# Feed-forward start of a decoder trunk: input block sums from two temporaries and a wide buffer, and their place in VectorE's queue

## The chip, the core and the metric

The kernel runs on one core of a Trainium2 chip. The metric is the time of one execution on the device in microseconds (us); the median of three runs is 2041.17 us (2040.91 to 2041.41). A profile of one further execution gives the rows that are quoted. PE is TensorE (its weight loads are PEld), DVE is VectorE, ACT is ScalarE, POOL is GpSimd, SP is the engine whose queue issues most DMAs. L475 is line 475 of the kernel before.

## What is computed

Two layers on a sequence of 512 tokens of width 1024, all in 32-bit floats. A layer is a half-step SwiGLU feed-forward block, a mixer (a convolution module in layer 0, sparse attention in layer 1), a second feed-forward block and a gated embedding; each block begins with an RMS norm.

```python
def rms_norm(x, g):
    return x * lax.rsqrt(jnp.mean(x * x, axis=-1, keepdims=True) + RMS_EPS) * g

def swiglu(x, wg, wu, wd):
    return (jax.nn.silu(x @ wg) * (x @ wu)) @ wd

for i in range(DEPTH):                       # DEPTH = 2
    x = x + 0.5 * swiglu(rms_norm(x, ffn1_norm[i]), ffn1_w_gate[i], ffn1_w_up[i], ffn1_w_down[i])
    ...                                      # conformer_conv or nsa_mixer
    x = x + 0.5 * swiglu(rms_norm(x, ffn2_norm[i]), ffn2_w_gate[i], ffn2_w_up[i], ffn2_w_down[i])
    ...                                      # gated embedding
```

The hidden width is 2816, which is 22 tiles of 128 columns. There are four feed-forward blocks in all: two in each layer.

## The kernel before

Activations lie transposed, features on the 128 partitions and 512 tokens along the row: `xs[k]`, k from 0 to 7, is 128 features of the residual stream. To keep 32-bit accuracy every operand is split into a high half, rounded by a copy on ACT, and a low half, the difference, taken on DVE; a product is then three matmuls, high x high, high x low and low x high (`mm3`, L349 to L351). Weight tiles of 128x1024 are loaded by SP's queue into `raw` (two buffers) or `rawx` (two buffers), then split into `wh` (ACT, L291 or L309) and `wl` (DVE, L292 or L310); there are five buffers of each. `ahead` (L327 on) does the loads and splits up to five steps before the product that uses them. The norm's factor is not applied to the inputs: the sum of squares runs along (`square_sum`, the running sum `acc` at L425), `rfin` sums it over features on PE (L438), adds the epsilon on DVE (`v`, L460, kept as `self.vins`), takes the power on POOL, spreads the row on PE and copies it to `R` on ACT (L451), and `R` scales the results.

A feed-forward block (`ffn`) takes its hidden tiles in three parts of 8, 8 and 6. Tiles 0 and 1 of the first part are plain: each has a gate and an up product of 8 input tiles. Their results are scaled by `R` (L576), go through SiLU on ACT (L577) into a temporary of tag `t` (four buffers), are multiplied (L551) and split (L553, L554). The SiLU frees one of the eight PSUM banks, the split another.

All other tiles go in pairs (`pairs`), with a scheme of the Strassen-Winograd kind: the product of a 2x2 block of weights with a 2x2 block of inputs is made from 7 products of half size instead of 8. It needs sums of weight blocks and sums of input blocks.

- Weight sums, per pair and once for gate and once for up. `_split` with kind "a" takes the first weight tile's halves (L291, L292) and calls `first_sums`, which makes `sq` (L320), a sum in `rawx` (L321) and its halves `s1hl` (L323, L324). `combine` with "c" and "d" makes the other two sums (L305, L306) and splits them (L309, L310). L305 and L306 read what the others wrote.
- Input sums, once per block: `right_sums` is called four times, for k = 0 to 3, and makes the four sums T1 to T4 of input tiles k and k+4. It scales the two tiles by the norm's gain on ACT (L473) into two temporaries `a` and `b`, makes `t12` and `t34` with four subtractions of 256 columns on DVE (L475 `t<-...`), and splits each into a `px` tile of 1024 (high half L483 on ACT, low half L475 `px<-t,px` on DVE). All four temporaries have tag `t`. The first pair needs them: its products run plain weights x inputs first (four), then T2 and T1, then T3, then T4.

`first_sums` of the first pair is called while tile 0's plain products are written out, that of the second pair when the first pair's are. Two calls of `right_sums` stand behind tile 0's products, two behind tile 1's, each within `issue_after(self.vins)`.

The order on each engine's queue is not the written order. A planner simulates the program and gives each engine the ready instruction that was written first; a `high_priority` block counts as written earlier. Within `issue_after(ins)`, the instructions that run on the engine of `ins` are queued behind it, without a wait for its end; instructions on other engines are free. Each engine then works through its queue in order, waiting by semaphores. A tag's buffers are used in turn, and a new tile waits for the users of the one that had its place.

The pairs' outputs are evicted from PSUM into tiles of tag `G`, 128x1024, three buffers (L496 on ACT, L495 on DVE): two for each pair.

Of the kernel before, what the change touches and what calls it, by code (L numbers as in the profile page):

```python
# [3 lines left out]

# [1 line left out]

# [5 lines left out]
F32 = mybir.dt.float32  # L12
F32R = mybir.dt.float32r
I32 = mybir.dt.int32
AF = mybir.ActivationFunctionType
OP = mybir.AluOpType
# [4 lines left out]
KD, FT = D // 128, DFF // 128  # L21
# [29 lines left out]
G, HPG, HD, KV, QD = 4, 4, 64, 256, 1024  # L51
# [143 lines left out]
class Kern:  # L195
# [72 lines left out]
    def _split(self, what, j):  # L268
        nc = self.nc
        w = sum(x[2] for x in UNITS[j])  # L270
        if what == "r":
            t = self.wpool.tile([128, HU], F32, name=f"wr{j}", tag="wh", bufs=self.HLB)
            nc.sync.dma_start(t[:, :w], self.a["w"][j, :, :w])
            self.hl[j] = (t, t)
            return
        if what in "cd":
            self.combine(what, j)
            return
        pair = KINDS[j] == "a"
        t = self.raw[j]  # L280
        if KINDS[j] == "s":
            del self.raw[j]
        h, l = self.halves()
        name = UNITS[j][0][0][0]
        nsa, calm = name.startswith("nsa"), name.startswith(CALM)
        eng = nc.gpsimd if calm or nsa and j % 4 in L_POOL else nc.vector
        for c in self.pieces(j, w):
            if nsa and j % 4 in H_POOL:
                nc.gpsimd.tensor_copy(h[:, c], t[:, c])
            else:  # L290
                nc.scalar.activation(h[:, c], t[:, c], AF.Copy)  # L291
            eng.tensor_tensor(l[:, c], t[:, c], h[:, c].bitcast(F32), op=OP.subtract)  # L292
        self.hl[("s", j) if pair else j] = (h, l)
        if pair:
            self.first_sums(j)

    def combine(self, what, j):

# [169 lines left out]
    def right_sums(self, name, i, k):  # L468

        nc = self.nc  # L470
        a, b, t12, t34 = (self.tmp() for _ in range(4))
        for t, kk in ((a, k), (b, k + 4)):
            nc.scalar.activation(t, self.xs[kk], AF.Copy, scale=self.col(name, i * KD + kk))  # L473
        lo, hi = slice(0, 256), slice(256, 512)
        sub = lambda o, x, y: nc.vector.tensor_tensor(o, x, y, op=OP.subtract)  # L475
        sub(t12[:, lo], a[:, hi], a[:, lo])
        sub(t12[:, hi], b[:, hi], t12[:, lo])
        sub(t34[:, lo], b[:, hi], a[:, hi])
        sub(t34[:, hi], b[:, lo], t12[:, hi])
        T = []  # L480
        for t in (t12, t34):
            p = self.ptile("px", 8, HU, F32R)
            nc.scalar.activation(p[:, :512], t, AF.Copy)  # L483
            sub(p[:, 512:], t, p[:, :512].bitcast(F32))
            T += [(p[:, :256], p[:, 512:768]), (p[:, 256:512], p[:, 768:])]
        self.T4.append(T)

    def pairs(self, names, i, f):
# [47 lines left out]
    def ffn(self, n, i, nxt):  # L536
        nc = self.nc
        X = self.X
        g, u, d = (f"ffn{n}_w_{s}" for s in ("gate", "up", "down"))
        self.now, self.T4 = (f"ffn{n}", i), []  # L540
        fin = self.rfin(self.acc)

        def plain(p, nm, f, ks=range(KD)):
            for k in ks:
                self.mm3(p, self.block((nm, i, k, f)), X[k], k == 0, k == KD - 1)

        for pi, fs in enumerate(PARTS):
            hid = {}

            def gated(f, gr, pu):  # L550
                nc.vector.tensor_tensor(pu, pu, gr, op=OP.mult)  # L551
                h, l = self.ptile("hid", HIDS, dt=F32R), self.ptile("hid", HIDS, dt=F32R)
                nc.scalar.activation(h, pu, AF.Copy)  # L553
                nc.vector.tensor_tensor(l, pu, h.bitcast(F32), op=OP.subtract)  # L554
                hid[f] = (h, l)

            if pi == 0:
                assert PLAIN == 2
                wait = []
                for f in range(PLAIN):  # L560
                    pg, pu = self.bank(), self.bank()
                    for ks in (range(KD - 1), (KD - 1,)) if f == 0 else (range(KD),):
                        plain(pg, g, f, ks)
                        if f == 1:
                            next(fin)
                        plain(pu, u, f, ks)
                    wait.append((f, pg, pu))
                    if f == 0:
                        next(fin)
                    with self.tc.issue_after(self.vins):  # L570
                        for k in (2 * f, 2 * f + 1):
                            self.right_sums(f"ffn{n}_norm", i, k)
                R = self.R
                for f, pg, pu in wait:
                    gr = self.tmp()
                    nc.vector.tensor_tensor(pg, pg, R, op=OP.mult)  # L576
                    nc.scalar.activation(gr, pg, AF.Silu)  # L577
                    gated(f, gr, pu)
            for f in fs[::2]:
                if f < PLAIN:  # L580
                    continue
                both = self.pairs((g, u), i, f)
                G = next(both)
                nc.vector.tensor_tensor(G, G, R[:, None, :].to_broadcast([128, 2, 512]), op=OP.mult)
                nc.scalar.activation(G, G, AF.Silu)
                U = next(both)
                drain(both)
                for h in range(2):
                    gated(f + h, G[:, h], U[:, h])
                self.skew_next()  # L590
                self.skew_next()
            last = pi == len(PARTS) - 1
            if last:
                self.prep_start(*nxt)
            for ms in ((0, 1), *((m,) for m in range(2, KD))):
                p = {m: self.bank() for m in ms}
                if len(ms) > 1:
                    self.held = {ENTRY[PLACE[d, i, f, m][0]] for f in fs for m in ms}
                for part in (fs[:-2], fs[-2:]):
                    for m in ms:  # L600
                        for f in part:
                            self.mm3(p[m], self.block((d, i, f, m)), hid[f], f == fs[0], f == fs[-1])
                self.held = set()
                for m in ms:
                    nc.vector.scalar_tensor_tensor(p[m], p[m], 0.5, R, op0=OP.mult, op1=OP.mult)  # L605
                    nc.vector.tensor_tensor(self.xs[m], p[m], self.xs[m], op=OP.add)
                    if last:
                        self.prep(m)
# [72 lines left out]
    def taps(self, c):  # L681

        T = [self.ptile("tw", TWB, 128 * LAGS) for _ in range(PH)]
        for q in range(PH):
            self.nc.sync.dma_start(T[q], self.a["tw"][CONV_ON[:c].count("pe"), q])
        return T

# [818 lines left out]
```

## Time and profile before

| | |
|---|---|
| median of three runs | 2041.17 us (2040.91 to 2041.41) |
| the profiled execution | 2038.98 us, its span 2037.2 us |
| PE busy | 1998.5 us, 98% of the span |
| DVE busy | 1564.8 us, 77% |
| ACT busy | 1102.2 us, 54% |
| POOL busy | 329.9 us, 16% |
| `wl<-raw,wh` on DVE (L292), 128x1024 | 203 x 1233 ns |
| `px<-t,px` on DVE (L475), 128x512 | 32 x 686 ns |
| `t<-...` on DVE (L475), 128x256 | 64 x 420 ns |

A row of a timeline gives the start and duration in us, the engine, the line, the operation, the tile written and the tiles read, and the size; in brackets stand the idle time of the engine just before it and what ended that. A row of a group gives the number of instructions, their busy time in us and the mean in ns of one. A row of a stretch gives the stretch in us, its length, then the busy time of each engine with the number of its instructions, the granted clock of PE (1.00 is full speed), the busy share of the DMA engines and the rate in GB/s. An instruction's duration includes its latency: on DVE and ACT the next one starts before it ends.

### The profile page before, as it was taken

The page shows a single profiled execution, that of the slowest core. Times are in us where ns is not written, and L with a number is a line of the kernel's source. Part 1 is how long each engine was busy: PE and PEld are TensorE (multiplying, and loading weights), DVE is VectorE, ACT ScalarE, POOL GpSimd, SP SyncE. Part 2 cuts the span into 40 slices and gives each one's busy share as a digit, 9 for nine tenths or more (in the row PEclk, how much of TensorE's full clock was granted, in tenths as well). Part 3 has the DMA queues.
Part 4 walks back from the last instruction along what each step waited for, and adds up shares of the span by engine and source line. Part 5 has one row for each costly group of instructions (what it writes and reads, how often), then busy time and mean ns, then how long its engine had stood idle before and what let it go on. Part 6 is the DMA issues. An engine that isn't in the chain of part 4 may idle for free.

```text
span 2037.2 us, 32829 instructions
## 1 busy us (share of the span) xinstructions
PE 1998.5 (98%) x12534; PEld 1794.0 (88%) x12534; DVE 1564.8 (77%) x2767; ACT 1102.2 (54%) x1972; POOL 329.9 (16%) x365
## 2 busy tenths in 40 slices
PE   8999999999999999999999999999999989999998
PEld 6989999888789898988899989888888779898987
DVE  8869777795687796877977868647989797786875
ACT  6636445663565363545644535437888665363543
POOL 0000000352200000021000000557666200000022
PEclk9999999999999999999999999999999999999999
DMA  4323323466325243243232322463332023232241
GB/s 168 104 93 103 125 75 103 180 213 204 125 98 172 92 143 118 96 144 104 83 114 94 114 91 89 159 189 108 90 93 100 27 98 114 94 115 93 88 142 61
DMA packets 79484, 235.16 MB, mean 115 GB/s; under 512 B 8848, under 2 KB 16160, under 8 KB 79328
## 3 DMA queue, kind: packets, MB, share of 16 engines
q1 hardware_dynamic: 78368, 230.69, 34.2%
q8 instruction: 98, 1.61, 0.3%
q0 software_dynamic: 816, 2.33, 0.3%
q14 instruction: 58, 0.48, 0.1%
q10 hardware_dynamic: 144, 0.07, 0.0%
HBM read 214.66 MB, written 16.29 MB: 113 GB/s over the span
## 4 chain that ended last, share of the span: by engine, by line
PE 83%; DVE 9%; ACT 3%; issue 2%; DMA 2%; SPq 0%; POOL 0%; DVEq 0%; ACTq 0%; POOLq 0%
PE b L349 26%; PE b L350 26%; PE b L351 26%; PE b L797 2%; DMA raw<-in_w 1%; DVE t L1221 1%; DVE wl L292 1%; PE b L1156 1%; PE b L1095 1%; DVE t L475 1%; DVE s L408 1%; DVE wl L310 1%; PE b L1218 1%; DVE e L1174 1%; ACT e L1176 0%
## 5 line engine op out<-in xcount | busy, mean ns | idle before, releaser
L349 PE MATMUL b<-s,wh 128*128 128x256 f32 (+1 forms) x1408 | 451.3, 322 | 8.3 <-ACT t L577 6.9
L350 PE MATMUL b<-s,wh 128*128 128x256 f32 (+1 forms) x1408 | 449.8, 320 | 1.3 <-DVE s L408 0.9
L351 PE MATMUL b<-s,wl 128*128 128x256 f32 (+1 forms) x1408 | 449.0, 320 | 0.1
L291 ACT ACTIVATE wh<-raw 128x1024 fp32r<-128x1024 f32 (+1 forms) x251 | 263.9, 1054 | 259.1 <-PE b L350 170.0
L349 PE MATMUL b<-px,wh 128*128 128x256 f32 (+1 forms) x1112 | 321.1, 290 | 6.0 <-ACT px L483 6.0
L350 PE MATMUL b<-px,wh 128*128 128x256 f32 (+1 forms) x1112 | 321.9, 290 | 2.3 <-DVE px L475 2.3
L351 PE MATMUL b<-px,wl 128*128 128x256 f32 (+1 forms) x1112 | 321.6, 290 | 0.0
L292 DVE TENSOR_TENSOR wl<-raw,wh 128x1024 fp32r<-128x1024 f32 (+1 forms) x205 | 251.4, 1228 | 74.9 <-ACT wh L291 74.2
L349 PEld LDWEIGHTS b<-s,wh 128*128 128x128 f32 x1408 | 270.1, 192 | 28.4 <-ACT t L577 7.8
L350 PEld LDWEIGHTS b<-s,wh 128*128 128x128 f32 x1408 | 270.3, 192 | 19.9 <-DVE s L408 2.2
L351 PEld LDWEIGHTS b<-s,wl 128*128 128x128 f32 x1408 | 270.0, 192 | 17.7 <-DVE wl L292 0.5
L351 PE MATMUL b<-hid,wl 128*128 128x512 f32 x704 | 275.3, 393 | 0.0
L350 PE MATMUL b<-hid,wh 128*128 128x512 f32 x704 | 275.1, 392 | 0.0
L349 PE MATMUL b<-hid,wh 128*128 128x512 f32 x704 | 270.4, 390 | 0.0
L292 POOL TENSOR_TENSOR wl<-raw,wh 128x1024 fp32r<-128x1024 f32 (+1 forms) x53 | 128.4, 2427 | 717.2 <-ACT wh L291 717.1
L349 PEld LDWEIGHTS b<-px,wh 128*128 128x128 f32 x1112 | 209.5, 189 | 10.9 <-ACT px L483 6.4
L350 PEld LDWEIGHTS b<-px,wh 128*128 128x128 f32 x1112 | 209.8, 189 | 7.5 <-DVE px L475 2.7
L351 PEld LDWEIGHTS b<-px,wl 128*128 128x128 f32 x1112 | 209.5, 189 | 3.8
L496 ACT ACTIVATE G<-b 128x256 f32<-128x256 f32 x400 | 145.0, 376 | 124.2 <-PE b L351 102.6
L605 DVE SCALAR_TENSOR_TENSOR b<-b,R 128x512 f32<-128x512 f32 x96 | 66.4, 694 | 120.3 <-PE b L351 120.3
L350 PEld LDWEIGHTS b<-hid,wh 128*128 128x128 f32 x704 | 132.3, 188 | 28.8
L349 PEld LDWEIGHTS b<-hid,wh 128*128 128x128 f32 x704 | 132.3, 188 | 28.6
(246 smaller groups left out, 3716.2 us busy)
## 6 DMA issues: line engine op xcount, KB each, us to landing
raw<-in_w SPq DMA_DIRECT2D x255, 512.0 KB, 3.3
rawx<-in_w SPq DMA_DIRECT2D x80, 512.0 KB, 3.2
tw<-in_tw SPq DMA_DIRECT2D x20, 576.0 KB, 6.7
skew<-table SPq DMA_DIRECT2D x16, 320.0 KB, 5.6
z<-t SPq DMA_DIRECT2D x16, 256.0 KB, 2.2
hid<-z SPq DMA_DIRECT2D x16, 256.0 KB, 4.1
tt<-skew SPq DMA_DIRECT2D x16, 256.0 KB, 3.0
wr<-in_w SPq DMA_DIRECT2D x8, 512.0 KB, 4.0
```

The source lines that it names most:

```text
L291: nc.scalar.activation(h[:, c], t[:, c], AF.Copy)
L292: eng.tensor_tensor(l[:, c], t[:, c], h[:, c].bitcast(F32), op=OP.subtract)
L310: nc.vector.tensor_tensor(l, src, h.bitcast(F32), op=OP.subtract)
L349: mm(out, sh, mh, start=start, stop=False, **how)
L350: mm(out, sh, ml, start=False, stop=False, **how)
L351: mm(out, sl, mh, start=False, stop=stop, **how)
L408: b = nc.vector.scalar_tensor_tensor(view(l), x, g, view(h.bitcast(F32)), op0=OP.mult, op1=OP.subtract)
L475: sub = lambda o, x, y: nc.vector.tensor_tensor(o, x, y, op=OP.subtract)
L496: copy = lambda o, x: nc.scalar.activation(o, x, AF.Copy)
L605: nc.vector.scalar_tensor_tensor(p[m], p[m], 0.5, R, op0=OP.mult, op1=OP.mult)
L797: nc.tensor.matmul(p[:, q * SP:q * SP + SP], T[q][:, d * 128:d * 128 + 128], u[:, q, o:o + SP], start=d == 0, stop=d == LAGS - 1)
L1095: nc.tensor.matmul(P[mh][:, :124], w, B[kk // 4][:, kk % 4, :], start=kk == 0, stop=kk == 15)
```

## The change

Three things change.

`right_sums` scales its two input tiles into the two halves of one tile of tag `G`, 1024 wide, and holds its sums in two temporaries instead of two inputs and two sums in four. The sums are laid out as T1 beside T3 and T2 beside T4. T1 and T3 are each a difference of neighbouring blocks, so one subtraction of 512 columns over a strided view makes both; T2 and T4 take one of 256 each. The splits into `px` are as before. The last low half's instruction is kept as `self.righted`.

The four calls stand within `issue_after(self.vins)` only in the very first feed-forward block; in the other three they are free.

From the time that all four calls are written out in a block (`len(self.T4) == 4`), the DVE instructions of `_split` for a pair's first tile (L292) and all DVE instructions of `first_sums` (L320, L321, L324) are queued behind `self.righted`. The first pair's are written before that and stay free; the second pair's are the first that this holds.

```diff
@@ _split
-            eng.tensor_tensor(l[:, c], t[:, c], h[:, c].bitcast(F32), op=OP.subtract)
+            with self.behind() if pair else nullcontext():
+                eng.tensor_tensor(l[:, c], t[:, c], h[:, c].bitcast(F32), op=OP.subtract)
         self.hl[("s", j) if pair else j] = (h, l)
         if pair:
-            self.first_sums(j)
+            with self.behind():
+                self.first_sums(j)
+
+    def behind(self):
+
+        return self.tc.issue_after(self.righted) if len(self.T4) == 4 else nullcontext()
@@ right_sums
-        a, b, t12, t34 = (self.tmp() for _ in range(4))
-        for t, kk in ((a, k), (b, k + 4)):
-            nc.scalar.activation(t, self.xs[kk], AF.Copy, scale=self.col(name, i * KD + kk))
+        ab, t13, t24 = self.ptile("G", 3, 1024), self.tmp(), self.tmp()
+        for n, kk in enumerate((k, k + 4)):
+            nc.scalar.activation(ab[:, n * 512:n * 512 + 512], self.xs[kk], AF.Copy, scale=self.col(name, i * KD + kk))
         lo, hi = slice(0, 256), slice(256, 512)
         sub = lambda o, x, y: nc.vector.tensor_tensor(o, x, y, op=OP.subtract)
-        sub(t12[:, lo], a[:, hi], a[:, lo])
-        sub(t12[:, hi], b[:, hi], t12[:, lo])
-        sub(t34[:, lo], b[:, hi], a[:, hi])
-        sub(t34[:, hi], b[:, lo], t12[:, hi])
-        T = []
-        for t in (t12, t34):
+        cut = lambda t: t.rearrange("p (h c) -> p h c", h=2)
+        sub(cut(t13), cut(ab)[:, :, hi], cut(ab[:, :512]))
+        sub(t24[:, lo], ab[:, 768:], t13[:, lo])
+        sub(t24[:, hi], ab[:, 512:768], t24[:, lo])
+        T = [None] * 4
+        for n, t in enumerate((t13, t24)):
             p = self.ptile("px", 8, HU, F32R)
             nc.scalar.activation(p[:, :512], t, AF.Copy)
-            sub(p[:, 512:], t, p[:, :512].bitcast(F32))
-            T += [(p[:, :256], p[:, 512:768]), (p[:, 256:512], p[:, 768:])]
+            self.righted = nc.vector.tensor_tensor(p[:, 512:], t, p[:, :512].bitcast(F32), op=OP.subtract).ins
+            T[n], T[n + 2] = ((p[:, c], p[:, 512 + c.start:512 + c.stop]) for c in (lo, hi))
@@ ffn
+                first = (n, i) == (1, 0)
...
-                    with self.tc.issue_after(self.vins):
+                    with self.tc.issue_after(self.vins) if first else nullcontext():
                         for k in (2 * f, 2 * f + 1):
                             self.right_sums(f"ffn{n}_norm", i, k)
```

More of the change, by code (lines that the diff above doesn't have):

```diff
@@ L2 @@
 import math
-from contextlib import ExitStack
+from contextlib import ExitStack, nullcontext
 import numpy as np
```

## The prediction

> **What bounds the kernel now.** I read the page first, then the busy time of TensorE in stretches of 20 us, then the timeline of PE, DVE and ACT where PE had gaps. PE is busy nearly all the span, so only its gaps and its slow clock are for sale. Apart from the attention layer and the last 17 us they lie at one place: the start of each of the four feed-forward blocks, where PE goes from the plain products to the first pair. I call these starts A (first block of layer 0), B (second block of layer 0), C and D (the same of layer 1). The stretches, with the columns PE, PEld, DVE, ACT, POOL, clock, DMA share, GB/s:
>
> ```profile
> span 2037.2 us, 32829 instructions
> ...
> 20.00:70.00 50.00, 43.76 (x288) 40.38 (x288) 46.96 (x75) 33.04 (x52) 1.14 (x1) 0.90 0.30 96
> 560.00:625.00 65.00, 63.77 (x418) 57.34 (x417) 58.11 (x91) 41.54 (x67) 1.71 (x2) 1.00 0.36 118
> 960.00:1010.00 50.00, 45.31 (x283) 41.44 (x282) 41.82 (x71) 30.52 (x48) 1.12 (x1) 0.93 0.20 67
> 1640.00:1680.00 40.00, 34.81 (x236) 32.40 (x236) 38.08 (x65) 26.36 (x43) 1.13 (x1) 0.96 0.25 79
> ```
>
> DVE is busy 46.96 of 50 us in A and 38.08 of 40 in D: at these starts DVE, not PE, carries the load. The gaps themselves, from PE's timeline (start, duration, then in brackets the idle time ahead and what ended it): first the wait for A's norm, which the change leaves alone, then two rows of A, one of B, three of C, two of D:
>
> ```profile
> 22.53 1.05 PE L438 MATMUL b<-meanr,acc 128*128 128x1 f32 x8 [2.08 <-DVE acc L425]
> ...
> 50.12 0.80 PE L349 MATMUL b<-px,wh 128*128 128x256 f32 x2 [3.44 <-ACT px L483]
> ...
> 52.06 0.58 PE L349 MATMUL b<-s,wh 128*128 128x256 f32 x1 [0.72 <-ACT t L577]
> ...
> 602.77 0.39 PE L349 MATMUL b<-s,wh 128*128 128x256 f32 x1 [1.14 <-ACT t L577]
> ...
> 989.85 0.39 PE L350 MATMUL b<-px,wh 128*128 128x256 f32 x1 [0.99 <-DVE px L475]
> ...
> 993.59 0.51 PE L349 MATMUL b<-px,wh 128*128 128x256 f32 x2 [2.54 <-ACT px L483]
> ...
> 995.50 0.58 PE L349 MATMUL b<-s,wh 128*128 128x256 f32 x1 [1.17 <-ACT t L577]
> ...
> 1662.00 0.39 PE L350 MATMUL b<-px,wh 128*128 128x256 f32 x1 [1.29 <-DVE px L475]
> ...
> 1667.11 0.58 PE L349 MATMUL b<-s,wh 128*128 128x256 f32 x1 [3.90 <-ACT t L577]
> ```
>
> Every gap but the first waits for the right sums (their high halves, L483, or low halves, L475) or for the SiLU of the plain products (L577), which frees a PSUM bank. Idle: A 3.44 + 0.72 = 4.2 us, B 1.1, C 0.99 + 2.54 + 1.17 = 4.7, D 1.29 + 3.90 = 5.2; 15.2 together. PE first ran dry at 50.12 - 3.44 = 46.7 in A, 989.85 - 0.99 = 988.9 in C and 1662.00 - 1.29 = 1660.7 in D. Behind the gaps PE runs at half clock, in steps of 3.41 us:
>
> ```profile
> 24.91:28.32 3.41, 3.41 (x10) 2.63 (x8) 3.41 (x9) 2.81 (x4) 1.14 (x1) 0.50 0.03 7
> ...
> 48.80:52.22 3.42, 1.38 (x5) 1.09 (x5) 3.26 (x8) 2.72 (x4) 0.00 (x0) 0.50 0.01 2
> 52.22:55.63 3.41, 3.41 (x16) 3.41 (x17) 3.00 (x5) 2.44 (x6) 0.00 (x0) 0.50 0.02 5
> ...
> 994.30:997.71 3.41, 2.24 (x11) 2.21 (x11) 2.68 (x5) 2.92 (x6) 0.00 (x0) 0.50 0.01 2
> 997.71:1001.12 3.41, 3.41 (x18) 3.41 (x17) 2.32 (x6) 2.83 (x8) 0.00 (x0) 0.50 0.00 0
> ...
> 1666.70:1670.10 3.40, 2.99 (x14) 2.99 (x15) 3.40 (x8) 2.50 (x6) 0.00 (x0) 0.50 0.00 0
> ```
>
> Half of the busy time there is lost: A (1.38 + 3.41)/2 = 2.4, C (2.24 + 3.41)/2 = 2.8, D 2.99/2 = 1.5, B nothing (clock 1.00 in its stretch). So A is worth 6.6 us, B 1.1, C 7.5 and D 6.7: 21.9 in all, the ceiling.
>
> Why the right sums are late is seen on DVE in C:
>
> ```profile
> 967.98 1.23 DVE L292 TENSOR_TENSOR wl<-raw,wh 128x1024 fp32r<-128x1024 f32 x1 [2.82 <-ACT wh L291]
> ...
> 985.76 0.69 DVE L320 TENSOR_TENSOR sq<-raw,rawx 128x512 f32<-128x512 f32 x1
> ...
> 987.03 1.22 DVE L292 TENSOR_TENSOR wl<-raw,wh 128x1024 fp32r<-128x1024 f32 x1
> 988.16 0.69 DVE L321 TENSOR_TENSOR rawx<-rawx 128x512 f32<-128x512 f32 x1
> ...
> 989.70 0.69 DVE L320 TENSOR_TENSOR sq<-raw,rawx 128x512 f32<-128x512 f32 x1
> 990.30 0.69 DVE L305 TENSOR_TENSOR sq<-rawx,raw 128x512 f32<-128x512 f32 x1
> 990.90 0.43 DVE L475 TENSOR_TENSOR t<-t 128x256 f32<-128x256 f32 x1
> 991.24 0.69 DVE L475 TENSOR_TENSOR px<-t,px 128x512 fp32r<-128x512 f32 x1
> 991.84 0.70 DVE L321 TENSOR_TENSOR rawx<-rawx 128x512 f32<-128x512 f32 x1
> ...
> 993.11 0.70 DVE L305 TENSOR_TENSOR sq<-rawx,raw 128x512 f32<-128x512 f32 x1
> ...
> 995.48 0.70 DVE L551 TENSOR_TENSOR b<-b,t 128x512 f32<-128x512 f32 x1 [0.73 <-ACT t L577]
> 996.08 0.68 DVE L475 TENSOR_TENSOR px<-t,px 128x512 fp32r<-128x512 f32 x1
> ```
>
> The last low half of the right sums starts at 996.08. Ahead of it, while PE stands, DVE does the second pair's first weight sums: two L320, two L321, two L305 and an L292. PE needs them only after the first pair's products.
>
> **The change, part by part.** Neighbours on DVE overlap: starts 0.60 us apart for 512 elements (990.30 to 990.90), 0.34 for 256 (990.90 to 991.24), 1.13 for 1024 (987.03 to 988.16).
>
> *Second pair's sums behind the last right sum.* Six at 0.60 plus 1.13 is 4.7 us, moved out from in front of the right sums in each block. L305 carries no edge of its own; it reads what L321 writes, so it goes along. A and D have the same L320 pair (groups of 40 to 54 us and of 1658.8 to 1669.4 us), D with 1.0 us of waiting for a weight load in front of it, which moves too; then the last low halves of A and D:
>
> ```profile
> L320 DVE TENSOR_TENSOR sq<-raw,rawx 128x512 f32<-128x512 f32 x2 | 1.4, 692 | 0.0
> ...
> L320 DVE TENSOR_TENSOR sq<-raw,rawx 128x512 f32<-128x512 f32 x2 | 1.4, 693 | 1.0 <-DMA rawx<-in_w 1.0
> ...
> 52.65 0.68 DVE L475 TENSOR_TENSOR px<-t,px 128x512 fp32r<-128x512 f32 x1
> ...
> 1668.22 1.29 DVE L475 TENSOR_TENSOR px<-t,px 128x512 fp32r<-128x512 f32 x2
> ```
>
> Behind the held instructions stand, on DVE, the second pair's splits L310 and the later sums; who waits for these is PE at the second pair, and the queue of SP, whose next loads need the raw tiles freed. No DMA is added or removed.
>
> *One subtraction fewer.* Four of 256 become one of 512 and two of 256: 4 x 0.34 = 1.36 against 0.60 + 0.68 = 1.28, so 0.08 us for each of 16 calls, 0.3 us in a block. The wide one has strided operands, which no row shows by itself; bounds are the 512 row (0.69) and the 1024 row (1.22), I take the 512 row because the element count is equal; the other end costs 4 x 0.5 = 2.1 us in a block.
>
> *Two temporaries and a wide buffer.* Four temporaries per call out of four made every call, and the SiLU's output, wait for the call before it. Now a call takes two, and the SiLU reuses one of the third call. The wide buffer has three places, shared with the pairs' outputs: the first pair's evictions then wait for calls two and three. Those calls are done ahead of PE's need in C (the stall there starts at the third), so I price the new wait at 0; at worst, bounded by one call on DVE (0.60 + 0.68 + two low halves at 0.60 = 2.5 us), it hits once a block.
>
> *Not held for the norm's addition* (B, C, D). In C the first call's two scaled inputs were ready by 963.6:
>
> ```profile
> 962.26 1.32 ACT L473 ACTIVATE t<-s,small 128x512 f32<-128x512 f32 x2
> ```
>
> DVE then idled 2.82 us in front of 967.98; a first call of 2.5 us fits. I take 2.8 for C and nothing for the others. The other end: a call that goes first delays the norm's running sum by one started instruction, 0.6 us in each of three blocks, 1.8.
>
> When is the last right sum done? A: 52.65 + 0.68 = 53.3, less 4.7, less one L551 (0.6) that goes behind, less 0.3: 47.7. C: 996.08 + 0.68 = 996.8, less 4.7, less L551 and its idle (0.60 + 0.73), less 0.3, less 2.8: 987.7. D: 1668.22 + 1.29 = 1669.5, less 4.7, less L551 0.6, less 0.3, less 1.0: 1662.9. To this comes ACT's share:
>
> ```profile
> 50.12 1.28 ACT L577 ACT_TABLE_LOAD   x1
> 51.41 0.60 ACT L577 ACTIVATE t<-b 128x512 f32<-128x512 f32 x1
> 51.91 0.62 ACT L483 ACTIVATE px<-t 128x512 fp32r<-128x512 f32 x1
> ```
>
> The function table's load and a SiLU stand in front of the last high half in A, 51.91 - 50.12 = 1.8 us. With its output free sooner the SiLU may go ahead of the last right sums, which can cost 0 to 1.8; I take 0.9 in A, C and D. (The Trainium skill, "ScalarE: Activation LUTs", section "What ACT_TABLE_LOAD costs", gives 1283 ns plus a drain of 1380 ns for a switch; by it the upper end would be 1.4 us more. This trace shows the SiLU 1.29 us after the load's start, so no such drain.)
>
> What stays of the gaps: A 47.7 + 0.9 - 46.7 = 1.9 us, so 2.3 of 4.2 are won; of the two half-clock steps I keep one whole (1.7 of 2.4), 0.7 won. B: the bank's release comes sooner, 1.1 won. C: 988.6 is ahead of 988.9, so all 4.7 and 2.8 won. D: 1662.9 + 0.9 - 1660.7 = 3.1 left, 2.1 won, the clock's 1.5 stays. Sum: 3.0 + 1.1 + 7.5 + 2.1 = 13.7 us. The profiled execution took 2038.98 (its span is 2037.2), which becomes 2025.3; it lay 2.2 below the median of 2041.17, against which the forecast is 2041.2 - 13.7 = **2027.5 us**. The ends of the unknown costs, one at a time: SiLU at 0 gives A and D 0.9 each, 2025.7; SiLU at 1.8 in three blocks 2030.2; the norm delayed 2029.3; the wide subtraction at the 1024 rate, 2.1 in three blocks, 2033.8; the wide buffer's wait in three blocks 2035.0. The two dearest together take the gain away, 2041.3.
>
> **The rivals.**
> *All of it goes.* The right sums are dense on DVE once nothing else fills in, and first-pair splits also go behind them. Then A and D close too: 2041.2 - 21.9 = 2019.3. For it: the four-temporary chain was itself a wait. Against: DVE is busy 38.08 of 40 us in D.
>
> *The gap left costs no half clock.* The granted clock halves after a gap of 1.29 + 3.90 in D, and 24.91 is half clock after the single gap of 2.08 us in front of 22.53; so gaps of 1.9 and 3.1 should. If they did not, A wins 1.7 more and D 1.5: 2041.2 - 16.9 = 2024.3. The Trainium skill, "TensorE: Matmul & The Clock Gate", section "HAM oscillation — how this bites in real kernels", has the rule that only gaps over about 3.4 us cost the clock; the row at 24.91 speaks against it.
>
> *The wait moves to the second pair.* DVE's work is only reordered; what it gives back for good is idle and savings: C 2.8 + 0.7 + 0.3, D 1.0 + 0.3, A and B 0.3 each, 5.7 us, time 2035.5. For it: DVE has 3 us idle in 50 in A. Against: after each start PE shows no gap, so DVE has run ahead there.
>
> *Slower: held sums behind a right sum that is not earlier.* If the last right sum stays put, because its ACT copies stand in ACT's queue behind weight copies that wait for PE, the second pair's first L292 comes 4.7 us later than now, with PE already out of work. Three blocks (A, C, D) lose 4.7 less 1.9 of idle in all: 14.1 - 1.9 = 12.2, time 2053.4. It decides from the point where the last right sum moves by less than 2.5 us, half of 4.7. Against: with a third buffer ACT's inputs come earlier.
>
> *It does not do what it says.* The instruction order is a planner's; if its plan had already put the sums elsewhere than the trace's order suggests, or stretched other stages by as much, nothing is left: 2041 within 4.
>
> **How the numbers follow.** Forecast 0.50, all goes 0.12, no half clock 0.08, moves to the second pair 0.12, slower 0.10, nothing 0.08. About 0.2%, 4.1 us, is what a measurement of this kernel tells from no change. The first four are faster, 0.82, of which I give 0.02 to "same" for costs at their dear ends; "nothing" may lean to slower by 0.01. So faster 0.80, same 0.09, slower 0.11. The range is to leave out 2 in 10: from 2018.5, a little below the ceiling's 2019.3, to 2041, where the two dearest ends meet; this leaves out the slower case and part of the empty one. The likeliest case by itself spans 2025.7 to 2035.0.
>
> **What would show it.** In the changed profile no L320, L321 or L292 of the second pair stands in front of the last L475-type low half in any block; the last of these ends near 47.7 in A and, against the block's start, 9 us earlier in C and 6.6 in D. PE's gaps sum to some 5 us instead of 15.2 at the four starts, clock 1.00 in C's stretch. I am wrong if PE gets a new gap of over 2 us at a second pair's product waiting for L292, L310 or L324, or if the wide subtraction takes nearer 1.2 than 0.69 us.

## The result and the profile after

The changed kernel took 2023.59 us (median of 4, 2022.71 to 2025.88) against 2041.04 (4 runs, 2040.54 to 2041.41) for the kernel before in the same comparison: ratio 0.9916, 95% interval 0.9904 to 0.9929, so 17.5 us or 0.84% faster. The forecast was 2027.5, 3.9 us above the measurement, in a range of 2018.5 to 2041.0.

The head and the first group of the changed kernel's page:

```profile
span 2020.9 us, 32801 instructions
...
PE 1992.9 (99%) x12534; PEld 1788.8 (89%) x12534; DVE 1558.5 (77%) x2751; ACT 1102.1 (55%) x1972; POOL 331.7 (16%) x365
```

PE is busy 5.6 us less than before (its work is the same, less of it at half clock), and the span is 16.3 us shorter. The starts A to D in stretches of the changed kernel; B, C and D are taken 8, 10 and 18 us earlier than before, so that each start lies inside:

```profile
20.00:70.00 50.00, 46.64 (x321) 43.19 (x320) 49.60 (x77) 34.21 (x54) 1.41 (x1) 0.97 0.28 91
552.00:617.00 65.00, 65.00 (x411) 57.93 (x410) 57.76 (x86) 39.82 (x63) 1.97 (x2) 1.00 0.36 118
950.00:1000.00 50.00, 49.76 (x324) 45.32 (x323) 46.71 (x75) 33.74 (x54) 1.39 (x1) 1.00 0.26 86
1622.00:1662.00 40.00, 38.65 (x251) 34.65 (x251) 39.17 (x64) 27.09 (x44) 1.42 (x1) 1.00 0.25 85
```

PE's idle time in C falls from 4.69 of 50 us to 0.24, in B from 1.23 of 65 to nothing, in D from 5.19 of 40 to 1.35. The clock is 1.00 in C and D. In A 3.36 us stay, and DVE is busy 49.60 of 50 us. PE's timeline shows where what is left lies (the row at 45.98 is the first product with a right sum, with no wait):

```profile
8.99 0.50 PE L355 MATMUL b<-s,wh 128*128 128x512 f32 x1 [1.95 <-ACT s L413]
...
26.25 0.94 PE L444 MATMUL b<-meanr,acc 128*128 128x1 f32 x7 [3.36 <-DVE acc L431]
...
45.98 0.28 PE L355 MATMUL b<-px,wh 128*128 128x256 f32 x1
...
987.38 0.38 PE L355 MATMUL b<-px,wh 128*128 128x256 f32 x1 [0.24 <-ACT G L502]
...
1650.33 0.39 PE L355 MATMUL b<-s,wh 128*128 128x256 f32 x1 [0.29 <-ACT wh L291]
...
1653.34 0.39 PE L356 MATMUL b<-px,wh 128*128 128x256 f32 x1 [0.81 <-DVE px L490]
1654.31 0.38 PE L355 MATMUL b<-px,wh 128*128 128x256 f32 x1 [0.24 <-ACT G L502]
```

All waits for the SiLU are gone. The prediction left gaps of some 5 us at the four starts; 0.24 us in C and 1.34 in D are left, 1.6 together. In A what is left is the wait for the norm, which grew from 2.08 to 3.36 us. DVE's timeline, the last low half of the right sums (now L490) in A with its neighbours, then in C and D:

```profile
49.80 0.69 DVE L557 TENSOR_TENSOR b<-b,t 128x512 f32<-128x512 f32 x1
50.40 0.68 DVE L490 TENSOR_TENSOR px<-t,px 128x512 fp32r<-128x512 f32 x1
50.99 1.22 DVE L293 TENSOR_TENSOR wl<-raw,wh 128x1024 fp32r<-128x1024 f32 x1
...
984.95 0.68 DVE L490 TENSOR_TENSOR px<-t,px 128x512 fp32r<-128x512 f32 x1
...
1652.60 0.68 DVE L490 TENSOR_TENSOR px<-t,px 128x512 fp32r<-128x512 f32 x1
```

The second pair's first L293 (L292 before) stands behind it in all four blocks, as written. The gain by stage is read from the last scaled result of the block (L605 before, L612 after), first before, then after:

```profile
147.34 0.70 DVE L605 SCALAR_TENSOR_TENSOR b<-b,R 128x512 f32<-128x512 f32 x1 [2.94 <-PE b L351]
...
695.53 0.70 DVE L605 SCALAR_TENSOR_TENSOR b<-b,R 128x512 f32<-128x512 f32 x1 [2.94 <-PE b L351]
...
1091.65 0.70 DVE L605 SCALAR_TENSOR_TENSOR b<-b,R 128x512 f32<-128x512 f32 x1 [2.94 <-PE b L351]
...
1762.40 0.70 DVE L605 SCALAR_TENSOR_TENSOR b<-b,R 128x512 f32<-128x512 f32 x1 [2.94 <-PE b L351]
```

```profile
144.50 0.70 DVE L612 SCALAR_TENSOR_TENSOR b<-b,R 128x512 f32<-128x512 f32 x1 [2.94 <-PE b L357]
...
690.99 0.70 DVE L612 SCALAR_TENSOR_TENSOR b<-b,R 128x512 f32<-128x512 f32 x1 [2.94 <-PE b L357]
...
1079.61 0.70 DVE L612 SCALAR_TENSOR_TENSOR b<-b,R 128x512 f32<-128x512 f32 x1 [2.94 <-PE b L357]
...
1746.41 0.70 DVE L612 SCALAR_TENSOR_TENSOR b<-b,R 128x512 f32<-128x512 f32 x1 [2.94 <-PE b L357]
```

The changed kernel is 2.84 us ahead after A, 4.54 after B, 12.04 after C and 15.99 after D. So A won 2.84 (forecast 3.0), the stretch with B 1.70 (1.1), that with C 7.50 (7.5) and that with D 3.95 (2.1).

A's figure is a balance of two. The first product with a right sum starts at 45.98 (above); before it started here:

```profile
42.28 0.28 PE L349 MATMUL b<-px,s1hl 128*128 128x256 f32 x1
```

That is 3.7 us later; from there to the end of the block it is 105.06 us before and 98.52 after, 6.5 less, nearly the ceiling of 6.6. What came late is the norm. The rows are ACT's scaled inputs of the right sums, its first square (L429) and DVE's addition of the norm, first of the kernel before, then of the changed one:

```profile
19.67 1.32 ACT L473 ACTIVATE t<-s,small 128x512 f32<-128x512 f32 x2
...
25.58 0.15 DVE L460 TENSOR_SCALAR v<-b 128x4 f32<-128x4 f32 x1
```

```profile
5.46 0.73 ACT L479 ACTIVATE G<-s,small 128x512 f32<-128x512 f32 x1 [0.92 <-DMA s<-in_xT]
...
17.49 0.62 ACT L429 ACTIVATE acc<-s 128x512 f32<-128x512 f32 x1
...
29.84 0.15 DVE L466 TENSOR_SCALAR v<-b 128x4 f32<-128x4 f32 x1
```

The wide buffers are free from the start, so six of the eight scaled inputs run on ACT between 5.46 and 14.79 us (six times some 0.6 us), among the high halves that the first products read (L413) and ahead of the squares that make the norm. Before, they came behind the squares, whose temporaries have their tag. The first square starts at 17.49 instead of 13.61, and the norm's addition comes 4.3 us later. `issue_after(self.vins)` does not stop this: it holds DVE's part, not ACT's. PE also runs at half clock in another place than before; the changed kernel's stretches:

```profile
11.00:14.40 3.40, 3.40 (x8) 2.73 (x9) 2.68 (x4) 3.40 (x6) 0.00 (x0) 0.50 1.04 415
28.10:31.50 3.40, 3.40 (x10) 2.66 (x9) 3.40 (x7) 2.07 (x4) 1.41 (x1) 0.50 0.00 0
```

Behind the first pair's start in A there is no half clock any more.

The stage figures are those of one execution each, and the number of such steps of 3.4 us varies. In the run held everywhere (below), whose queue on DVE is the same in A, PE is at half clock from about 24.0 to 34.2 us, three steps in place of two, and A's block ends at 146.42 instead of 144.50: A's gain is 2.8 us in one execution and 0.9 in the other. D's stretch (from C's last scaled result to D's) takes 666.80 us in the changed kernel and 667.65 and 668.90 in two runs whose edit is in A alone, so that D's gain is 3.95 us in one execution and 3.10 and 1.85 in the others.

### The profile page after: what moved, and what is told of

Read it like the earlier page. It is cut to its first block, busy times and chain, and to the rows that moved or that the text cites. A ratio compares the mean times of both kernels' runs of the same rounds, so it can differ in the third digit from the quotient of the medians.

```text
span 2020.9 us, 32801 instructions
## 1 busy us (share of the span) xinstructions
PE 1992.9 (99%) x12534; PEld 1788.8 (89%) x12534; DVE 1558.5 (77%) x2751; ACT 1102.1 (55%) x1972; POOL 331.7 (16%) x365
## 4 chain that ended last, share of the span: by engine, by line
PE 88%; DVE 7%; ACT 3%; issue 1%; DMA 1%; SPq 0%; POOL 0%; DVEq 0%; ACTq 0%; POOLq 0%
PE b L355 27%; PE b L357 27%; PE b L356 27%; PE b L804 2%; DVE t L1228 1%; PE b L1163 1%; PE b L1102 1%; PE b L1225 1%; DVE s L414 1%; DVE acc L431 1%; ACT e L1183 1%; PE b L1244 0%; DMA raw<-in_w 0%; DVE e L1181 0%; PE b L1245 0%
## 5 line engine op out<-in xcount | busy, mean ns | idle before, releaser
L293 DVE TENSOR_TENSOR wl<-raw,wh 128x1024 fp32r<-128x1024 f32 (+1 forms) x205 | 251.1, 1226 | 65.7 <-ACT wh L291 65.1
L293 POOL TENSOR_TENSOR wl<-raw,wh 128x1024 fp32r<-128x1024 f32 (+1 forms) x53 | 128.4, 2430 | 709.6 <-ACT wh L291 709.5
L357 PEld LDWEIGHTS b<-hid,wl 128*128 128x128 f32 x704 | 132.2, 188 | 27.5
```

The lines of the kernel that those rows point to most:

```text
L357: mm(out, sl, mh, start=False, stop=stop, **how)
```

## The experiments

The question was which of the three parts carries the gain. Where a run has the queueing or not (Q), the new form of `right_sums` or the four temporaries (T), and the three later blocks free or held (U), the medians are:

| T new form | U free | Q queued | us | ratio to before, 95% |
|---|---|---|---|---|
| no | no | no | 2040.7 to 2041.0 | 1 |
| no | no | yes | 2022.65 | 0.9893 to 0.9926 |
| yes | no | no | 2025.19 | 0.9911 to 0.9941 |
| no | yes | no | 2043.8 | 1.0005 to 1.0024 |
| yes | yes | no | 2022.47 | 0.9896 to 0.9925 |
| yes | no | yes | 2025.95 | 0.9911 to 0.9941 |
| no | yes | yes | 2032.62 | 0.9952 to 0.9976 |
| yes | yes | yes | 2023.59 | 0.9904 to 0.9929 |

**Without the queueing.** The changed kernel, second pair's sums not held:

```diff
-        return self.tc.issue_after(self.righted) if len(self.T4) == 4 else nullcontext()
+        return nullcontext()
```

> The changed kernel, but later pairs' weight sums are not queued behind the last right sum. Theory Q (the gain comes from moving the second pair's sums, 4.7 us of VectorE in each block, out from in front of the right sums): most of the gaps come back, some 2034 us. Rival T (the gain comes from two temporaries instead of four, which broke the chain of calls): the right sums are written before the second pair's sums and are now ready earlier, so the planner puts them first by itself, 2024 to 2027 us.

Measured 2022.47 us (0.9911, 0.9896 to 0.9925), the changed kernel's time. In A one L326 (at 51.02) and one L293 of the second pair now stand ahead of the last low half, and PE does not wait for it. DVE's timeline of this run:

```profile
52.22 1.22 DVE L293 TENSOR_TENSOR wl<-raw,wh 128x1024 fp32r<-128x1024 f32 x1
53.35 0.69 DVE L490 TENSOR_TENSOR px<-t,px 128x512 fp32r<-128x512 f32 x1
```

Given the other two parts, the queueing is worth nothing that can be measured.

**The queueing alone**, on the kernel before:

```diff
+            with self.behind() if pair else nullcontext():
+                eng.tensor_tensor(l[:, c], t[:, c], h[:, c].bitcast(F32), op=OP.subtract)
...
+            with self.behind():
+                self.first_sums(j)
...
-            sub(p[:, 512:], t, p[:, :512].bitcast(F32))
+            self.righted = sub(p[:, 512:], t, p[:, :512].bitcast(F32)).ins
```

> The kernel before, with only the queueing of later pairs' weight sums behind the last right sum. Theory Q: 2027 to 2031 us, all but the share of the free calls in C (2.8 us) and of the saved subtraction. Rival T: the chain of four temporaries keeps the last right sum late, VectorE idles instead of doing the sums, and the second pair comes late: 2041 us or more.

Measured 2022.65 us (0.991, 0.9893 to 0.9926): this part alone gives the whole gain, more than theory Q gave it. What it leaves on PE's timeline is the SiLU's wait in A, C and D, and short waits for a right sum in C (0.24 us) and D:

```profile
48.96 0.39 PE L355 MATMUL b<-s,wh 128*128 128x256 f32 x1 [1.20 <-ACT t L583]
...
985.24 0.39 PE L355 MATMUL b<-s,wh 128*128 128x256 f32 x1 [1.17 <-ACT t L583]
...
1649.83 0.51 PE L355 MATMUL b<-px,wh 128*128 128x256 f32 x2 [0.51 <-ACT px L489]
1651.74 0.39 PE L355 MATMUL b<-s,wh 128*128 128x256 f32 x1 [1.17 <-ACT t L583]
```

**Held for the norm in all blocks**, the rest as changed:

```diff
-                    with self.tc.issue_after(self.vins) if first else nullcontext():
+                    with self.tc.issue_after(self.vins):
```

> The changed kernel, but all four calls stay held for the norm's addition in every block. By the prediction only C loses: its last right sum comes 2.8 us later, 987.7 + 0.9 + 2.8 = 991.4 against 988.9, so a gap of about 2.5 us there, 2026 to 2028 us with the half clock behind it. Rival: VectorE's idle time in C was no loss, since the last right sum waits for ScalarE: 2023.6 us as the changed kernel.

Measured 2025.95 us (0.9926, 0.9911 to 0.9941), 2.4 above the changed kernel, with intervals that overlap. The gap of 2.5 us that was expected in C did not come: PE waits 0.23 us there for a right sum. With the run of the new form only (below), which holds as well, it makes a pair at 2025 to 2026 beside the free ones at 2022 to 2024.

**The first block's inputs behind the squares.** The changed kernel, with ACT's scaled inputs in A queued behind the norm's last square:

```diff
-        nc.scalar.activation(view(sq), x, AF.Square)
+        self.squared = nc.scalar.activation(view(sq), x, AF.Square).ins
...
-                    with self.tc.issue_after(self.vins) if first else nullcontext():
+                    with ExitStack() as queue:
+                        for ins in (self.vins, self.squared) if first else ():
+                            queue.enter_context(self.tc.issue_after(ins))
```

> The changed kernel, with the scaled inputs of the very first block also queued on ScalarE behind the last square of its norm. In the changed kernel's profile six of them (L479) stand among the norm's high halves (L413), PE's first product starts at 8.99 instead of 7.61 and the norm's addition at 29.84 instead of 25.58. Theory S (that cost the first block about 4 us): the norm's addition is back near 25.6, PE's wait for the running sum near 2.1, time 2019 to 2021 us. Rival: the right sums of that block are then late again and a gap comes back in their place: 2023 us or more.

Measured 2022.01 us (0.9907, 0.9892 to 0.9921), not to be told from the changed kernel. PE's timeline:

```profile
22.19 1.05 PE L444 MATMUL b<-meanr,acc 128*128 128x1 f32 x8 [1.18 <-DVE acc L431]
...
45.69 0.39 PE L355 MATMUL b<-s,wh 128*128 128x256 f32 x1 [0.71 <-ACT wh L291]
...
50.47 0.38 PE L356 MATMUL b<-px,wh 128*128 128x256 f32 x1 [0.81 <-DVE px L490]
```

The norm's wait shrinks from 3.36 to 1.18 us, so the order on ACT was its cause. Part of it comes back as 1.5 us of new gaps at the first pair: 0.71 us for a weight's high half on ACT, 0.81 for a right sum's low half on DVE.

**Only the free calls**, on the kernel before:

```diff
-                    with self.tc.issue_after(self.vins):
+                    with self.tc.issue_after(self.vins) if first else nullcontext():
```

> The kernel before, with only the calls freed from the norm's addition in the last three blocks (four temporaries, no queueing). By the prediction's terms only C gains, 2.8 us: 2038 us. Rival O (what matters is which of the two, right sums or second pair's sums, the planner writes first, and any push on the right sums tips it): 2026 to 2032 us, B, C and D gain most of what the changed kernel gains there, A nothing.

Measured 2043.8 us (1.0015, 1.0005 to 1.0024), a little slower. A and D keep their gaps. In C the old ones are gone, and another has come. Rows of POOL, PE and DVE in this run:

```profile
973.07 8.88 POOL L431 TENSOR_TENSOR r<-v,power 128x4 f32<-128x4 f32 x1 [35.75 <-DVE v L460]
...
982.00 1.11 PE L444 MATMUL b<-ident,r 128*128 128x128 f32 x4 [3.97 <-POOL r L431]
...
980.40 0.68 DVE L475 TENSOR_TENSOR px<-t,px 128x512 fp32r<-128x512 f32 x1
983.79 0.70 DVE L577 TENSOR_TENSOR b<-b,R 128x512 f32<-128x512 f32 x1 [2.71 <-ACT R L451]
```

The power of the norm on POOL, 128x4, takes 8.88 us instead of 1.12, and PE waits 3.97 us for it. DVE runs without a pause until 981.08; POOL ends at 981.95. B has the same (8.63 us, 3.58 of wait).

**Only the new form**, not queued, held in all blocks:

```diff
-        return self.tc.issue_after(self.righted) if len(self.T4) == 4 else nullcontext()
+        return nullcontext()
...
-                    with self.tc.issue_after(self.vins) if first else nullcontext():
+                    with self.tc.issue_after(self.vins):
```

> Only the new form of the input sums (two temporaries, wide buffer, one subtraction fewer), held in every block, nothing queued. The run without the queueing but with free calls lost nothing against the changed kernel. If the temporaries broke the chain (theory T): 2024 to 2027 us, as the run held everywhere. If it was the freeing of the calls: A as in the changed kernel, the others back, 2035 us or more.

Measured 2025.19 us (0.9926, 0.9911 to 0.9941). The new form by itself takes 15.5 us off, and leaves in B 0.61, in C 0.56, in D 0.46 us of gaps at the start.

**Free calls and queueing, with four temporaries:** the edits of the second and the fifth run together.

> The kernel before with free calls and the queueing, but with four temporaries. The run with the queueing alone gained 4.4 us up to the end of A's block (the changed kernel 2.8) and 5.8 in C's (7.5). If the terms add: C's 7.5 and A's 4.4, 2020 to 2021.5 us. Rival: with four temporaries the SiLU still waits for the last call, its gap of 1.2 us stays in C and D and the freeing wins nothing, 2022 to 2024 us.

Measured 2032.62 us (0.9964, 0.9952 to 0.9976), 10 us above the queueing alone. POOL in C, for which PE then waits 3.97 us:

```profile
968.93 8.88 POOL L437 TENSOR_TENSOR r<-v,power 128x4 f32<-128x4 f32 x1 [35.76 <-DVE v L466]
```

B again the same, 8.64 us and a wait of 3.92.

**Less work on DVE.** The fourth run's kernel, with the low half of the second plain up tile on POOL in every feed-forward block:

```diff
-        eng = nc.gpsimd if calm or nsa and j % 4 in L_POOL else nc.vector
+        first_up = name.startswith("ffn") and name.endswith("up") and UNITS[j][0][0][3] == 1
+        eng = nc.gpsimd if calm or first_up or nsa and j % 4 in L_POOL else nc.vector
```

> The run with the first block's inputs behind the squares, and in each block the low half of one plain weight tile (up, tile 1; L293, 1.13 us of VectorE) on GpSimd instead, where such a subtraction took 2.43 us in the profile of before. That run's gaps in A and D end with a low half on VectorE (0.81 and 0.84 us). If VectorE's queue sets them, they close: 2019 to 2021 us. Rival: the tile is needed before GpSimd is done, or VectorE slows beside it: 2022 us or more.

Measured 2039.87 us (0.9998, 0.9989 to 1.0007): 18 us lost against the fourth run, 8.9 in B's stretch and 8.9 in C's by the last scaled results. `r` took 11.32 us in B and 9.75 in C. In A, where `r` took 1.41 us, the waits for a low half did not close either (0.81 and 0.73 us). PE's rows in B and C:

```profile
585.97 1.12 PE L451 MATMUL b<-ident,r 128*128 128x128 f32 x4 [7.23 <-POOL r L438]
...
983.16 1.11 PE L451 MATMUL b<-ident,r 128*128 128x128 f32 x4 [5.91 <-POOL r L438]
```

**The norm's power off POOL**, in the run with free calls and queueing, and as a control in the changed kernel; both leave out the root, and write 1/v on DVE:

```diff
-            r = self.rsqrt(v, 4)
+            r = self.tiny.tile([128, 4], F32, name="r", tag="r")
+            self.nc.vector.reciprocal(r, v)
```

> The kernel of before with free calls and the queueing (2032.62, ratio 0.9964), but the power of the norm on DVE instead of POOL; to have a form that DVE takes, it writes 1/v in place of the inverse square root of v, 128x4, so the numbers are not those of the reference, and the instructions are as many. Theory P (the 10 us that free calls cost beside queueing alone are the two stays of POOL in r, 8.64 and 8.88 us, at B and C): the waits of PE for r of 3.9 us at 582 and 978 are gone, time 2022 to 2025. Rival O (free calls put the right sums ahead of other work, and POOL is slow only because it comes late anyway): PE waits as before at another instruction, time 2030 to 2034.

> The changed kernel with 1/v on DVE in place of the inverse square root on POOL: it leaves out the root, as a control for the run with free calls and queueing. In the changed kernel r takes 1.4 us on POOL, and PE does not wait for it at the four starts except in A. Expected by P: 0.3 to 1 us faster than the changed kernel in A, else the same: 2021.5 to 2024. A time of 2015 or less would say that r on POOL holds something also there, and that the control takes that much off whatever the form.

Measured 2021.24 us (0.9902, 0.9887 to 0.9917) where POOL's form took 2032.62, and 2025.94 (0.9923, 0.991 to 0.9935) in the control, no faster than the changed kernel and above the range that P gave it. PE's waits for `r` are gone in the first, and by the last scaled results B's stretch is 6.6 us shorter and C's 5.9. So the 10 us of free calls beside queueing were POOL's two long stays in `r`, and where `r` is short, moving it wins nothing.

**The old form in the first block only:**

```diff
+        if (name, i) == ("ffn1_norm", 0):
+            a, b, t13, t24 = (self.tmp() for _ in range(4))
+            for t, kk in ((a, k), (b, k + 4)):
+                nc.scalar.activation(t, self.xs[kk], AF.Copy, scale=self.col(name, i * KD + kk))
...
+        else:
...
```

> The changed kernel with the four temporaries of before in the very first feed-forward block only, new form in the other three, queueing in all. Theory H (the new form brings ACT's scaled inputs ahead of the norm's squares in A, which puts the norm 4.3 us later): v of the first block at 25.9 instead of 29.84, the end of A's stage at 143 instead of 144.5, time 1.5 to 1.9 less than the changed kernel, 2021.7. Rival (the norm's delay is hidden behind the right sums, which take what it leaves): the end of A's stage stays within 0.5 of 144.5 and the time is the changed kernel's.

Measured 2023.06 us (0.9911, 0.9897 to 0.9925). The norm's addition is at 25.99, as H said, but the block's last scaled result is at 144.29 beside 144.50: the rival's figure, though not by its reason. PE idles no more in A than with the queueing alone (2.15, 0.74 and 0.24 us from the norm on, there 2.12 and 1.20), and that run ends A at 142.95. What differs is the clock: 0.50 from 23.5 to 30.3 us here, two steps, and from 24.5 to 27.9 there, one; a step costs half of 3.4, 1.7 us. The start of A has the SiLU's wait back:

```profile
23.02 1.51 PE L444 MATMUL b<-meanr,acc 128*128 128x1 f32 x8 [2.15 <-DVE acc L431]
...
49.74 0.39 PE L355 MATMUL b<-s,wh 128*128 128x256 f32 x1 [0.74 <-ACT t L593]
```

**Four narrow subtractions in the new form:**

```diff
-        sub(cut(t13), cut(ab)[:, :, hi], cut(ab[:, :512]))
+        sub(t13[:, lo], ab[:, 256:512], ab[:, :256])
         sub(t24[:, lo], ab[:, 768:], t13[:, lo])
+        sub(t13[:, hi], ab[:, 768:], ab[:, 256:512])
```

> The changed kernel with the wide strided subtraction of 512 columns made as two of 256; all else as in the changed kernel. By the prediction's price the wide one saves 0.08 us of DVE in each of 16 calls, 0.3 us in a block, and none of it stands where PE waits: 2023 to 2025, no difference that can be measured. Rival (DVE is what the starts A and D wait for, so the 0.3 us come back whole, with the half clock): 1 to 2 us slower, and gaps of 0.3 us more in A and D.

Measured 2031.95 us (0.9955, 0.9942 to 0.9967), 8.4 above the changed kernel, which neither side expected. POOL and PE of this run:

```profile
965.37 10.15 POOL L437 TENSOR_TENSOR r<-v,power 128x4 f32<-128x4 f32 x1 [35.72 <-DVE v L466]
...
975.58 1.11 PE L450 MATMUL b<-ident,r 128*128 128x128 f32 x4 [5.20 <-POOL r L437]
...
1662.27 0.39 PE L355 MATMUL b<-s,wh 128*128 128x256 f32 x1 [2.08 <-ACT G L503]
```

In C POOL stays in `r` for 10.15 us and PE waits 5.20 for it; in D a wait for a PSUM eviction (2.08 us) is new. By the last scaled results 7.2 of the 8.4 us are lost in C's stretch. So the wide subtraction is worth 8 us here, but hardly through DVE's time: in the changed kernel's order `r` happens to be short (1.39 us in C). This form was not run with `r` off POOL.

No run beats the changed kernel by more than the intervals tell apart.

## Why the prediction was right, and where it was not

**The bound.** Right: the gaps and the half clock at the four starts were what was for sale. Of the ceiling of 21.9 us, 17.5 came; with the new form and the queueing C gave its whole 7.5.

**The second pair's sums behind the right sums** (4.7 us a block). Half right. The step works as worked out: by itself it takes the time to 2022.65, 18 us. But it was made the only carrier, and it is not needed: without it, with the other two parts, the time is 2022.47.

**Two temporaries and a wide buffer, priced at 0.** This is the step that failed most. Alone it is worth 15.5 us. The text named the reason itself, that four temporaries of four made each call and the SiLU's output wait for the call before, and then gave it no price, since the rows of DVE seemed to lay the delay on the second pair's sums. A row in front of a late instruction shows what filled the time, not what the instruction waited for. In the kernel before, the right sums' inputs waited for temporaries, and the planner put the sums that were ready in their place. Either edit undoes that: earlier right sums, or sums kept from the place. That both are enough is shown by the runs. That the chain of temporaries held the inputs is seen on ACT before: six of the scaled inputs in A, B and D wait for a subtraction on DVE, 7.0 us together, the longest in B:

```profile
588.12 0.73 ACT L473 ACTIVATE t<-s,small 128x512 f32<-128x512 f32 x1 [3.00 <-DVE t L475]
```

That these waits made the last right sums late is argued and not shown by itself: with the queueing alone ACT's scaled inputs still wait so, 6.1 us together, and PE waits 0.75 us for right sums.

**The wide buffer's other side.** The forecast looked for its cost in the pairs' evictions; it came in A as a norm 4.3 us later, through ACT. The prediction's 3.0 for A was met (2.84) by two errors that cancel, which is luck: all of the gap went (6.5 won where 3.0 was expected, with no wait for a right sum left), and the first product with a right sum came 3.7 us later. The old form there, or the inputs queued behind the squares, takes the norm's delay away, but the block ends only 0.2 and 0.8 us sooner (144.29 and 143.72). These ends follow the number of steps at half clock in A more than the sums. With one step A ends at 142.95 (queueing alone) and 143.72 (inputs behind the squares), with two at 144.29 (old form in the first block), 144.50 (changed kernel) and 144.70 (new form only), with three at 146.42 (held everywhere) and 146.91 (without the queueing). What sets the number is open: after waits for the norm of 2.12 and 2.15 us it was one and two.

**The end of the last right sum.** Forecast 47.7 in A, 987.7 in C, 1662.9 in D. Measured 51.1 (50.40 + 0.68), 985.6, 1653.3. The starts have moved: C's by 4.5 and D's by 12.0 us. With that put back C has 990.2 and D 1665.3, 2.5 and 2.4 us later than forecast; A is 3.4 later, with a norm 4.3 later. The last right sum moved less than I said, in part because the product of the SiLU (L557, L551 before), which I had put behind it, still stands in front of it (row at 49.80). PE does not suffer, because my left gap set the end of the last sum against the moment at which PE first ran dry, and that moment belongs to an earlier sum. In D PE waits for the last one from 1652.5 (1653.34 less 0.81); 1660.7 less 12.0 is 1648.7, so it had 3.8 us more work than I gave it. So D's gap left is 1.34 us (0.81 of it for a right sum), not 3.1, and no half clock follows it. C's 7.50 for a forecast of 7.5 is in part luck for the same reason: by the prediction's own sum 990.2 lies behind 988.9 and would have left a gap.

**D's sum.** Ceiling 6.7 less 1.3 is 5.4; 3.95 was measured for the stretch. The rest is at the end of the attention layer, where this execution of the changed kernel has one more step at half clock. Stretches before, then after:

```profile
1595.00:1598.40 3.40, 2.98 (x10) 2.36 (x10) 1.77 (x8) 3.33 (x14) 3.40 (x8) 0.51 0.01 2
```

```profile
1584.60:1588.00 3.40, 2.82 (x10) 1.93 (x10) 2.41 (x7) 3.26 (x11) 3.40 (x9) 0.50 0.00 0
1588.00:1591.40 3.40, 3.21 (x11) 2.10 (x9) 2.94 (x9) 1.80 (x6) 1.55 (x4) 0.50 0.01 2
```

Half of 3.21 is 1.6 us. The change edits nothing in that layer; why the clock stayed low for one step more is not shown.

**ACT's share** (0.9 in A, C and D). Too much: in the changed kernel the table load starts some 6 us ahead of the last high half (43.63 and 49.58 in A, 978.13 and 984.08 in C), and only the second SiLU stands directly in front of it in C and D, 0.48 us from start to start; no product waits for the SiLU. With four temporaries and queueing the SiLU's wait does stay, 1.17 to 1.20 us in A, C and D, so the new form removes it, as the text held possible.

**One subtraction fewer.** The wide one takes 0.68 us by the trace (`t<-G`, 128x512), as priced at 0.69. Its effect on the time, 8.4 us, runs through POOL's `r`, a way the prediction did not have.

**Not held for the norm** (2.8 in C, other end 1.8 lost). Right in place and too large in size: with the new form C's stretch (from B's last scaled result to C's) takes 388.6 and 389.0 us with free calls, 390.4 and 390.8 with held ones, 1.8 us. In the whole time it is 2.4 and 2.7 us, intervals overlapping. With four temporaries it costs, 3 us alone and 10 beside the queueing, by a long `r` on POOL instead of by the norm's running sum.

**The rivals.** "All of it goes" was right for the gaps of B and C, and nearly for D. "Moves to the second pair" and "slower" fell: no product of the second pair waits for a weight sum. "The gap left costs no half clock" gave 2024.3, the nearest figure of all, but by luck: no gap of its size was left behind the starts, so it was not put to the test. In A the clock halves at 28.10 after a wait of 3.36 us, which the Trainium skill's rule (over about 3.4 us, "TensorE: Matmul & The Clock Gate", section "HAM oscillation — how this bites in real kernels") does not tell from its bound; at 11.00 it halves after one of 1.95 us, with shorter ones around it, against the rule.

## What to carry to other kernels

When two instructions compete for an engine, ask what the late one waited for (buffers first) before laying its delay on those that stand in front of it: a tag whose buffers all go to one call makes a chain, and a planner fills the hole with what is ready. Two cures of one stall do not add up; test each alone before crediting one. A buffer that comes free earlier lets work run ahead on every engine that writes it, so look there for what it pushes back; here holding that work brought the norm forward again, but no time that could be measured. Before comparing the ends of stages, count the steps at half clock in each execution.

## What was not expected of the hardware

A 128x4 operation on POOL took 1.01 to 1.43 us at most norms and 8.63 to 11.32 us in seven places, B and C of the three runs above (free calls alone, free calls and queueing, low half on POOL) and C of the one with narrow subtractions. In each of the seven POOL ends 0.86 to 0.90 us after DVE's unbroken row of subtractions and additions does (981.08 to 981.95 in C of the run with only the free calls). The Trainium skill, "SBUF — State Buffer", section "🔬 SBUF: two separate sides", says that a DVE instruction with two SBUF inputs and a POOL instruction that reads SBUF lock one pair of ports against each other: whichever starts first holds it for its whole instruction, and the other waits. The seven ends agree with a lock. But a lock for one instruction would let POOL in after at most the longest, 1.22 us, and in the seven places it is kept out over thirteen of them or more. In the changed kernel and before, DVE is as dense and POOL gets in behind the first instruction:

```profile
964.05 1.39 POOL L437 TENSOR_TENSOR r<-v,power 128x4 f32<-128x4 f32 x1 [35.45 <-DVE v L466]
```

What decides between the two is open: in C the low-half run has the same three kinds of DVE instruction behind `v` as the changed kernel has, and there `r` took 9.75 us.
